# FFN down-projections as seven half-size products, one normalised and split input per FFN, two weight sums by adding transfers, the embedding in the second FFN

## The chip, the cores and the metric

The kernel runs on one core of one Trainium2 chip. The metric is the time of one execution on the device, in microseconds (us); the time of a kernel is the median of its runs. Five engines work side by side: PE (matrix products; its weight loads are listed apart as PEld), DVE and POOL (elementwise), ACT (copies, scalings and functions) and SP (issues transfers). Tiles are 128 partitions high; "128x512" is 128 partitions by 512 float32 numbers.

## The reference

One decoder layer on 512 tokens of width 1024, in float32: a first feed-forward half step, a token mixer, a second feed-forward half step, and a gated embedding. Cut to what the change touches:

```python
def rmsnorm(x, g):
    return x * lax.rsqrt(jnp.mean(x * x, axis=-1, keepdims=True) + EPS) * g

def swiglu(h, w_gu, w_down):              # w_gu 1024 x 5632, w_down 2816 x 1024
    g, u = jnp.split(h @ w_gu, 2, axis=-1)
    return (jax.nn.silu(g) * u) @ w_down

x = x + 0.5 * swiglu(rmsnorm(x, ffn1_norm[i]), ffn1_wgu[i], ffn1_wdown[i])
...
x = x + merged @ w_out[i]                 # attention, convolution and their gates
x = x + 0.5 * swiglu(rmsnorm(x, ffn2_norm[i]), ffn2_wgu[i], ffn2_wdown[i])
e = rmsnorm(p[i] @ ple_proj[i], ple_norm[i])
gate = jax.nn.sigmoid(rmsnorm(x, ple_gate_norm[i]) @ ple_gate_w[i])
x = x + gate * e
```

## The kernel before

**Layout.** x lies feature-major in eight tiles `x[o]` of 128x512: features down the partitions, the 512 tokens along the row. Every product keeps float32 accuracy by splitting both sides into a high and a low part: `split_into` (line 681) makes the high part on ACT (an ACTIVATE copy with rounding, `whi`) and the low part on DVE (a subtraction, `wlo`), and `mm3` (line 708) issues three matmuls: low weights by high data, high by high, high weights by low data. A weight piece is a tile of 128x1024, loaded by one SP transfer (`raw_...`) and split.

**Stages.** In program order: the first FFN (call on line 1104), the mixer, whose steps stand in the table ORDER (line 40; K and Q projections, a and b the convolution inputs, A E V attention, g and h gates, p its projection, L a norm, e0 e1 the embedding), two projections `cp` and `wo`, the second FFN (line 1476), and the gate `pg` with the output.

**An FFN** (`ffn`, line 920) has 22 blocks of 128 hidden features. The first four (f1) or two (f2) are plain: `products` runs `f_g` and `f_u` over eight k tiles on the normalised-later input `h` (gain applied, the token norm `rb` multiplied in afterwards by `gated`). The other blocks go two at a time through `pair` (line 966): a 2 by 2 block product (two feature blocks by two halves of the model width, and the two halves of the tokens) done as seven products of half the row length instead of eight, each on a form of the weights and a form of the input, numbered 1 to 7. Weight forms 1, 2 and 4 are loaded pieces; 3, 5, 6 and 7 are sums `f_s` of pieces, made by eight "flex" additions of 128x512 per pair that the planner puts on POOL or DVE. `sums` (line 895) makes the input sums `f_t` from x before the norm is known, so each output is multiplied by `rb` after the products. One pair is 7 forms x 2 outputs (gate and up) x 4 k tiles x 3 = 168 matmuls of 128x256.

`down` (line 1059) follows after blocks 0 to 8, 8 to 16 and 16 to 22. It takes the gated blocks, split by `act_split` (line 930) into tiles of the slot class "o", and for each of the eight outputs runs 3 x 8 (or 3 x 6) matmuls of 128x512 on one weight piece (`wd`), multiplies the result by `rb` (`f_d<-f_d,f_n_rb`) and adds half of it to `x[o]`. After the last chunk, `after(o)` splits the new x for the next norm, output by output. Two FFNs have 2 x 8 x (24 + 24 + 18) = 1056 such matmuls.

**What sets the order.** The program is recorded (`record`, line 652), and a planner (`passes`, `simulate`, lines 624 and 396) lists it out per engine with its own cost table (line 297), a due time for each instruction and a fixed number of slots per class of tile (SLOTS, line 649: 54 general "a", 4 "o", three each of raw weights, high and low parts, 8 PSUM banks, two "k"). Transfers are issued by SP when a raw slot is free. Each engine then runs its list in order, with semaphores between engines.

## Time and profile before

| | |
|---|---|
| runs | 1175.85, 1176.26, 1173.57 us; median 1175.85 |
| span of the profiled execution | 1172.4 us |
| PE, DVE, ACT, POOL busy | 1161.6, 973.4, 639.7, 456.2 us |
| matmuls of 128x512 and 128x256 in the order of PE | 3262 and 3288 |
| DMA engines, mean | 98 GB/s, 115.30 MB in all |

The profiled execution's own time isn't listed apart from its span; the median of the runs is 3.45 us above the span, and that difference stands for what lies around the span. The granted TensorE clock is at nine tenths or more in each of the 40 slices of the span. All instructions bear one line (L1522, the planner's emission loop), so groups are told apart by tile names: `f_d` is a down-projection's output, `wlo_wgu`/`whi_wgu` the parts of up-projection weights, `wlo_wd`/`whi_wd` those of down-projection weights, `f_s` weight sums, `f_t` input sums, `f_g` and `f_u` gate and up.

### The profile page before, as it was taken

How to read it: one execution, taken by the hardware profiler on the slowest of the kernel's cores; microseconds unless marked ns; L12 is line 12 of the kernel's file. 1: busy time of each engine (PE TensorE's matmuls, PEld its weight loads, DVE VectorE, ACT ScalarE, POOL GpSimd, SP SyncE). 2: the span in 40 equal slices, each digit the busy share in tenths (PEclk: the TensorE clock that was granted, in tenths of full speed). 3: DMA queues.
4: the chain of work that ended last, by engine and by line, in shares of the span. 5: the costliest groups of instructions: out<-in, count | busy, mean ns of one | idle time of the engine just before them, and what ended most of it. 6: DMA issues, size and time to landing. Idle time of an engine off the chain costs nothing.

```text
span 1172.4 us, 17962 instructions
## 1 busy us (share of the span) xinstructions
PE 1161.6 (99%) x6740; PEld 1029.6 (88%) x6740; DVE 973.4 (83%) x1481; ACT 639.7 (55%) x1139; POOL 456.2 (39%) x418
## 2 busy tenths in 40 slices
...
GB/s 226 146 85 96 126 75 106 99 136 76 82 104 100 90 91 37 108 55 72 76 89 106 88 94 93 105 96 102 107 104 132 74 86 100 121 127 41 104 108 72
DMA packets 37815, 115.30 MB, mean 98 GB/s; under 512 B 4704, under 2 KB 9440, under 8 KB 37728
## 3 DMA queue, kind: packets, MB, share of 16 engines
...
q10 hardware_dynamic: 144, 0.03, 0.0%
...
## 4 chain that ended last, share of the span: by engine, by line
PE 94%; ACT 2%; DVE 2%; POOL 1%; issue 1%; DMA 0%; SPq 0%; DVEq 0%; ACTq 0%
PE f_d L1522 20%; PE ap L1522 4%; PE ga L1522 4%; PE pg L1522 4%; PE cp L1522 4%; PE wo L1522 4%; PE ca L1522 3%; PE gb L1522 3%; PE cb L1522 3%; PE f_u L1522 2%; PE f_g L1522 2%; PE q1b L1522 2%; PE q0b L1522 2%; PE sc L1522 2%; PE f_u14b L1522 1%; PE f_u20b L1522 1%
## 5 line engine op out<-in xcount | busy, mean ns | idle before, releaser
L1522 POOL TENSOR_TENSOR f_s<-raw_wgu,raw_wgu 128x512 f32<-128x512 f32 x51 | 86.6, 1710 | 345.5 <-DMA raw_wgu<-in_wgu 115.6
L1522 POOL TENSOR_TENSOR y<-y,ct 128x507 f32<-128x507 f32 (+27 forms) x90 | 119.1, 1343 | 6.2 <-ACT ct L1522 4.6
L1522 ACT ACTIVATE whi_wgu<-raw_wgu 128x1024 fp32r<-128x1024 f32 (+1 forms) x93 | 76.2, 834 | 81.5 <-PE f_d L1522 29.5
L1522 DVE TENSOR_TENSOR wlo_wgu<-raw_wgu,whi_wgu 128x1024 fp32r<-128x1024 f32 (+1 forms) x93 | 105.1, 1140 | 7.8 <-ACT whi_wgu L1522 7.3
L1522 DVE SCALAR_TENSOR_TENSOR cz<-u,dww,cz 128x504 f32<-128x504 f32 (+25 forms) x145 | 104.7, 732 | 2.3
L1522 ACT ACTIVATE whi_wd<-raw_wd 128x1024 fp32r<-128x1024 f32 (+1 forms) x48 | 47.4, 987 | 103.9 <-PE f_d L1522 84.6
L1522 DVE TENSOR_TENSOR f_d<-f_d,f_n_rb 128x512 f32<-128x512 f32 x48 | 33.4, 697 | 75.8 <-PE f_d L1522 75.8
L1522 DVE TENSOR_TENSOR f_wl<-f_s,f_wh 128x512 fp32r<-128x512 f32 x72 | 71.4, 1012 | 1.5 <-ACT f_wh L1522 1.0
L1522 POOL TENSOR_TENSOR f_s<-raw_wgu,f_s 128x512 f32<-128x512 f32 x31 | 52.3, 1694 | 51.6 <-DVE f_us L1522 20.6
L1522 DVE TENSOR_TENSOR wlo_wgu<-f_s,whi_wgu 128x512 fp32r<-128x512 f32 x80 | 66.3, 863 | 6.0 <-ACT whi_wgu L1522 5.8
L1522 ACT ACTIVATE whi_wgu<-f_s 128x512 fp32r<-128x512 f32 x80 | 46.6, 625 | 32.4 <-PE f_d L1522 8.9
L1522 ACT ACTIVATE ct<-u,dww 128x505 f32<-128x505 f32 (+28 forms) x90 | 58.2, 701 | 2.2 <-DVE u L1522 2.1
L1522 ACT ACTIVATE f_wh<-f_s 128x512 fp32r<-128x512 f32 x72 | 43.6, 626 | 26.6 <-DVE f_s L1522 12.9
L1522 POOL TENSOR_TENSOR f_s<-f_s,raw_wgu 128x512 f32<-128x512 f32 x31 | 49.2, 1594 | 20.8 <-DVE f_s L1522 6.0
L1522 DVE TENSOR_TENSOR wlo_wd<-raw_wd,whi_wd 128x1024 fp32r<-128x1024 f32 (+1 forms) x48 | 54.1, 1128 | 3.8 <-ACT whi_wd L1522 3.6
L1522 ACT ACTIVATE f_gs<-f_gs 128x512 f32<-128x512 f32 x44 | 27.6, 629 | 34.8 <-DVE f_gs L1522 34.4
L1522 POOL TENSOR_TENSOR f_t<-x 128x256 f32<-128x256 f32 x8 | 6.5, 807 | 86.8 <-DVE x L1522 81.6
L1522 DVE SCALAR_TENSOR_TENSOR x<-f_d,x 128x512 f32<-128x512 f32 x48 | 32.9, 689 | 1.4
L1522 DVE TENSOR_TENSOR f_s<-raw_wgu,raw_wgu 128x512 f32<-128x512 f32 x25 | 32.9, 1319 | 0.0
L1522 ACT ACTIVATE s<-s,m,q_r 128x128 f32<-128x128 f32 x64 | 31.0, 491 | 0.5 <-DVE m L1522 0.4
L1522 ACT ACTIVATE whi_wzc<-raw_wzc 128x1024 fp32r<-128x1024 f32 x16 | 17.0, 1061 | 22.3 <-issue 8.4
L1522 ACT ACTIVATE whi_wzg<-raw_wzg 128x1024 fp32r<-128x1024 f32 x16 | 17.1, 1069 | 16.9 <-PE ga L1522 5.0
...
## 6 DMA issues: line engine op xcount, KB each, us to landing
raw_wgu<-in_wgu SPq DMA_DIRECT2D x80, 512.0 KB, 3.7
raw_wd<-in_wd SPq DMA_DIRECT2D x32, 512.0 KB, 3.5
raw_wzc<-in_wzc SPq DMA_DIRECT2D x16, 512.0 KB, 3.6
raw_wzg<-in_wzg SPq DMA_DIRECT2D x16, 512.0 KB, 3.6
...
raw_wq<-in_wq SPq DMA_DIRECT2D x8, 512.0 KB, 3.6
raw_wap<-in_wap SPq DMA_DIRECT2D x8, 512.0 KB, 3.6
```

The lines of the kernel that those rows point to most:

```text
L1522: getattr(engines[op.eng], op.what)(*a, **k)
```

## The change

- **Down-projections** become 2 by 2 block products as well: two halves of the outputs (`x[o]` and `x[o+4]`) by even and odd hidden blocks by the two halves of the tokens. `unit` holds the seven forms and serves both `pair` and `down`. The hidden blocks go in groups of 4, 4 and 3 pairs, each group in two units (outputs 0, 1, 4, 5 and 2, 3, 6, 7). A unit is 7 forms x 2 x np x 3 matmuls of 128x256: 168 for np = 4 pairs and 126 for np = 3. The results go straight from PSUM into x by additions of 128x256 (seven forms give 14 per unit), with no product by `rb`.
- **The gated blocks** are no longer split one by one: `act_forms` makes their four sums per pair (`ta`, `tb`, four flex additions of 128x256) and splits the seven forms.
- **The normalised input**: `sums` now multiplies x by gain and norm (`xn`, eight per FFN), splits it once (`nh`, `nl`) and makes the sums `f_t` from it. All pair products use it, so no output needs `rb` after that, and the first pair can't start before the norm. The plain blocks still use `h`.
- **Weight sums**: of four sums per unit, two (21+22, then 11+(21)) are made by transfers that POOL issues and that add the loaded piece onto the tile in place (`accum_op`); two (`s6`, `s3`) by four flex additions of 128x512.
- **The embedding** leaves the mixer's ORDER (where it stood between p1 and p6) and is recorded in the second FFN behind the pair of blocks 18 and 19.
- **Slots and planner**: a 70, raw, hi and lo 4 each, no class "o"; a cost and a duration for POOL's transfers; three mixtures for the due times are tried; weights of `wdown` laid out on the host in blocks.

Per engine, in the order of the changed kernel against that of before: PE 2206 matmuls of 128x512 (1056 fewer) and 5136 of 128x256 (1848 more); POOL issues 62 transfers (54 of 128x1024, 8 of 128x768), where it issued none of weights; SP issues as many as before.

The order of PE at the first down-projection, before (where output 0 ends and output 1 begins; `f1_a01h` holds the high parts of blocks 4 to 7 and `f1_a00h` of blocks 0 to 3, `wd10` and `wd11` are the weights of outputs 0 and 1):

```order
L1522 MATMUL f1_d0_0_1190<-f1_a01h_1027,wlo_wd10_1039 128x512
L1522 MATMUL f1_d0_0_1190<-f1_a01h_1027,whi_wd10_1003 128x512
L1522 MATMUL f1_d0_0_1190<-f1_a01l_1054,whi_wd10_1003 128x512
L1522 MATMUL f1_d0_1_1225<-f1_a00h_604,wlo_wd11_1102 128x512
L1522 MATMUL f1_d0_1_1225<-f1_a00h_604,whi_wd11_1050 128x512
L1522 MATMUL f1_d0_1_1225<-f1_a00l_685,whi_wd11_1050 128x512
```

and PE there now, the first form of the first unit (`wd10_0`: first FFN, group at pair 0, half 0; `f1_f0_1` holds high and low part of form 1 of the pair at block 0, "x2" are the two matmuls with the high weights):

```order
L1567 MATMUL wd10_0_b0_1711<-f1_f0_1_609,wlo_wd10_0_1_1689 128x256
L1567 MATMUL wd10_0_b0_1711<-f1_f0_1_609,whi_wd10_0_1_1652 128x256 x2
L1567 MATMUL wd10_0_b0_1711<-f1_f2_1_819,wlo_wd10_0_1_1689 128x256
L1567 MATMUL wd10_0_b0_1711<-f1_f2_1_819,whi_wd10_0_1_1652 128x256 x2
L1567 MATMUL wd10_0_b0_1711<-f1_f4_1_1132,wlo_wd10_0_1_1689 128x256
L1567 MATMUL wd10_0_b0_1711<-f1_f4_1_1132,whi_wd10_0_1_1652 128x256 x2
L1567 MATMUL wd10_0_b0_1711<-f1_f6_1_1262,wlo_wd10_0_1_1689 128x256
L1567 MATMUL wd10_0_b0_1711<-f1_f6_1_1262,whi_wd10_0_1_1652 128x256 x2
```

Each step is half as long, and one unit's products run over 7 forms instead of 8 blocks.

The order of POOL around the weights of blocks 8 and 9 of the first FFN, before (`f1_s0_8` to `f1_s3_8` are the four sums of this pair, cut in halves 0 and 1):

```order
L1522 TENSOR_TENSOR f1_s0_8_0_1408<-raw_wgu18_10_1380,raw_wgu18_11_1302 128x512
L1522 TENSOR_TENSOR f1_s2_8_0_1421<-raw_wgu18_00_1314,raw_wgu18_10_1380 128x512
L1522 TENSOR_TENSOR f1_s1_8_1_1442<-f1_s0_8_1_1414,raw_wgu18_00_1314 128x512
L1522 TENSOR_TENSOR f1_s2_8_1_1463<-raw_wgu18_00_1314,raw_wgu18_10_1380 128x512
L1522 TENSOR_TENSOR f1_s3_8_0_1479<-raw_wgu18_01_1347,f1_s1_8_0_1428 128x512
L1522 TENSOR_TENSOR f1_s3_8_1_1508<-raw_wgu18_01_1347,f1_s1_8_1_1442 128x512
```

and now (DMA rows are the adding transfers; `raw_wgu18_21`, `_11`, `_12` are this pair's loaded pieces, `wgu18_s6` and `wgu18_s3` its two sums; `f1_ta`, `f1_tb` the sums of gated blocks of earlier pairs):

```order
L1567 DMA raw_wgu18_21_993<-in_wgu1 128x1024
L1567 TENSOR_TENSOR f1_tb2_1064<-f1_ta2_831,f1_us3_972 128x256
L1567 TENSOR_TENSOR f1_ta4_1115<-f1_us4_729 128x256
L1567 TENSOR_TENSOR wgu18_s6_0_1180<-raw_wgu18_21_993,raw_wgu18_11_789 128x512
L1567 TENSOR_TENSOR wgu18_s3_0_1200<-raw_wgu18_12_1011,wgu18_s6_0_1180 128x512
L1567 DMA raw_wgu18_11_789<-in_wgu1 128x1024
L1567 TENSOR_TENSOR wgu18_s3_1_1227<-raw_wgu18_12_1011,wgu18_s6_1_1188 128x512
L1567 TENSOR_TENSOR f1_ta6_1268<-f1_us6_1037 128x256
L1567 TENSOR_TENSOR f1_ta4_1115<-f1_us5_821,f1_ta4_1115 128x256
L1567 DMA raw_wgu110_21_1237<-in_wgu1 128x1024
```

Three of the four weight additions stand on POOL here (the fourth is on DVE), two transfers are issued between them, and the sums of gated blocks have come in.

The order of DVE at the start of the second FFN, before (behind the last instruction of its norm, `f2_n_dgl`; `f2_gs0` and `f2_gs1` are the plain blocks):

```order
L1522 TENSOR_TENSOR f2_s1_2_0_8215<-f2_s0_2_0_8196,raw_wgu22_00_8035 128x512
L1522 TENSOR_TENSOR f2_s2_2_1_8225<-raw_wgu22_00_8035,raw_wgu22_10_8150 128x512
L1522 TENSOR_TENSOR f2_s3_2_1_8239<-raw_wgu22_01_8089,f2_s1_2_1_8220 128x512
L1522 TENSOR_TENSOR wlo_wgu22_2_8264<-raw_wgu22_01_8089,whi_wgu22_2_8232 128x1024
L1522 TENSOR_TENSOR wlo_wgu22_5_8276<-f2_s0_2_0_8196,whi_wgu22_5_8249 128x512
L1522 TENSOR_TENSOR wlo_wgu22_5_8276<-f2_s0_2_1_8202,whi_wgu22_5_8249 128x512
L1522 TENSOR_TENSOR f2_gs0_8294<-f2_g0_8053,f2_n_rb_8256 128x512
```

and now (behind the low part of the first weights, eight `f2_xn`, and the first two `f2_nl`; `nl` are low parts of the normalised input, `f2_t1` an input sum, `wlo_wgu22_2` and `_6` weights of forms 2 and 6):

```order
L1567 TENSOR_TENSOR f2_nl2_8741<-f2_xn2_8671,f2_nh2_8680 128x256
L1567 TENSOR_TENSOR f2_nl2_8741<-f2_xn3_8678,f2_nh2_8680 128x256
L1567 TENSOR_TENSOR wlo_wgu22_2_8747<-raw_wgu22_12_8522,whi_wgu22_2_8646 128x1024
L1567 TENSOR_TENSOR f2_nl4_8754<-f2_xn4_8688,f2_nh4_8698 128x512
L1567 TENSOR_TENSOR f2_nl5_8763<-f2_xn5_8695,f2_nh5_8712 128x512
L1567 TENSOR_TENSOR f2_nl6_8770<-f2_xn6_8704,f2_nh6_8718 128x512
L1567 TENSOR_TENSOR f2_nl7_8779<-f2_xn7_8714,f2_nh7_8726 128x512
L1567 SCALAR_TENSOR_TENSOR f2_t1_0_8786<-f2_t0_0_8668,f2_xn4_8688 128x256
L1567 SCALAR_TENSOR_TENSOR f2_t1_0_8786<-f2_t0_0_8668,f2_xn5_8695 128x256
L1567 SCALAR_TENSOR_TENSOR f2_t1_1_8796<-f2_t0_1_8683,f2_xn6_8704 128x256
L1567 SCALAR_TENSOR_TENSOR f2_t1_1_8796<-f2_t0_1_8683,f2_xn7_8714 128x256
L1567 TENSOR_TENSOR wlo_wgu22_6_8807<-wgu22_s6_0_8561,whi_wgu22_6_8757 128x512
```

The normalised input now stands on DVE between the norm and the weights of the first pair; before, the weights' low parts followed the norm at once.

The diff, cut to its core:

```diff
-g1 p0 p2 g7 p3 L0 p4 h3 p7 h2 p5 p1 e0 e1 p6 h5 h0 h6
+g1 p0 p2 g7 p3 L0 p4 h3 p7 h2 p5 p1 p6 h5 h0 h6
...
+PLAIN, OWN = (4, 2), (False, False)
+DOWNS = {10: [(0, 4)], 18: [(4, 8)], 20: [(8, 11)]}
...
-SLOTS = {"a": 54, "o": 4, "raw": 3, "hi": 3, "lo": 3, "ps": 8, "k": 2, "x": 8, "c": 100000}
+SLOTS = {"a": 70, "raw": 4, "hi": 4, "lo": 4, "ps": 8, "k": 2, "x": 8, "c": 100000}
...
-    def sums(tag, gain):
+    def sums(tag, gain, rb):
         t1, t2 = slice(0, HS), slice(HS, S)
+        xn, hn = [], []
+        for k in range(KD):
+            xn.append(ftile(f"{tag}_xn{k}"))
+            nc.vector.scalar_tensor_tensor(xn[k], x[k], gain[:, k : k + 1], rb, op0=ALU.mult, op1=ALU.mult)
+            n, c = (HS, HS * (k % 2)) if k < 4 else (S, 0)
+            if c == 0:
+                new = rtile(f"{tag}_nh{k}"), rtile(f"{tag}_nl{k}")
+            hn.append([t[:, c : c + n] for t in new])
+            split_into(*hn[k], xn[k][:, 0:n])
         forms = [[] for _ in range(4)]
         for q in range(KD // 4):
             vs = [ftile(f"{tag}_t{f}_{q}") for f in range(4)]
             for j in range(2):
                 k, v = 2 * q + j, [t[:, j * HS : (j + 1) * HS] for t in vs]
-                g1, g2 = gain[:, k : k + 1], gain[:, k + 4 : k + 5]
-                nc.gpsimd.tensor_tensor(v[0], x[k][:, t2], x[k][:, t1], op=ALU.subtract)
-                nc.scalar.activation(v[0], v[0], AF.Copy, scale=g1)
-                nc.scalar.activation(v[2], x[k][:, t2], AF.Copy, scale=g1)
...
+                a, b = xn[k], xn[k + 4]
+                nc.flex.tensor_tensor(v[0], a[:, t1], a[:, t2], op=ALU.subtract)
+                nc.flex.tensor_tensor(v[2], b[:, t2], a[:, t2], op=ALU.subtract)
+                for to, less, xs in ((1, 0, t2), (3, 1, t1)):
+                    nc.vector.scalar_tensor_tensor(v[to], v[less], -1.0, b[:, xs], op0=ALU.mult, op1=ALU.subtract)
-    def ffn(tag, wgu, wdown, h, gain, ss, after, cuts, wide, plain, own):
+        return forms, hn
+    lo_, hi_ = slice(0, HS), slice(HS, S)
+    def unit(name, src, n, col, forms, own=False, first=None):
+        A = {}
+        for b, cls in ((11, "raw"), (12, "raw"), (21, "raw"), (22, "k")):
+            A[b] = nc.tile(f"raw_{name}_{b}", [P, PIECE], F32, cls)[:, 0:n]
+            nc.behind = first if b == 22 else None
+            nc.sync.dma_start(A[b], src(b))
+            nc.behind = None
+        nc.gpsimd.dma_start(A[21], src(22), accum_op=ALU.add)
+        half = n // 2
+        sm = {f: [ftile(f"{name}_s{f}_{c}")[:, 0:half] for c in range(2)] for f in (6, 3)}
+        for c in range(2):
+            s = slice(c * half, (c + 1) * half)
+            nc.flex.tensor_tensor(sm[6][c], A[21][:, s], A[11][:, s], op=ALU.add)
+            nc.flex.tensor_tensor(sm[3][c], A[12][:, s], sm[6][c], op=ALU.add)
...
+        b1, b2 = ([ps_tile(f"{name}_{b}{m}")[:, lo_] for m in range(2)] for b in "ab")
+        def times(m, f, w, to, start):
+            with nc.group(f"{name}_p{f}_{m}"):
+                for k, x_ in enumerate(forms[f]):
...
+                    mm3(to[m], wk, x_, start and k == 0, k == len(forms[f]) - 1, skip=f in (3, 4, 6, 7))
+        for f1, f2 in ((1, 2), (6, 5), (7, 3)):
+            w1, w2 = form(f1), form(f2)
+            if f1 == 1:
+                nc.gpsimd.dma_start(A[11], src(21), accum_op=ALU.add)
+            for m in range(2):
+                times(m, f1, w1, b2, f1 == 1)
+                times(m, f2, w2, b1, f2 != 3)
+                yield f1, m, b1[m], b2[m]
+        w = form(4)
+        for m in range(2):
+            times(m, 4, w, b2, False)
+            yield 4, m, b1[m], b2[m]
...
+        def act_forms(i, u0, u1):
+            t1, t2 = ftile(f"{tag}_ta{i}"), ftile(f"{tag}_tb{i}")
+            nc.flex.tensor_tensor(t1[:, lo_], u0[:, lo_], u0[:, hi_], op=ALU.subtract)
+            nc.flex.tensor_tensor(t2[:, lo_], u1[:, hi_], u0[:, hi_], op=ALU.add)
+            nc.flex.tensor_tensor(t1[:, hi_], u1[:, hi_], t1[:, lo_], op=ALU.subtract)
+            nc.flex.tensor_tensor(t2[:, hi_], t1[:, hi_], u1[:, lo_], op=ALU.subtract)
+            one = rtile(f"{tag}_f{i}_1")
+            split_into(one[:, lo_], one[:, hi_], u0[:, lo_])
+            f = {1: (one[:, lo_], one[:, hi_])}
+            for n1, n2, v, sign in ((2, 3, u1, -1.0), (5, 6, t1, None), (7, 4, t2, -1.0)):
+                hi, lo = split(f"{tag}_f{i}_{n1}", v, sign)
+                f[n1], f[n2] = ((hi[:, t], lo[:, t]) for t in (lo_, hi_))
+            acts.append(f)
...
-            add(0, A[1, 0], A[1, 1], ALU.add)
-            add(1, sm[0], A[0, 0], ALU.subtract)
-            add(3, A[0, 1], sm[1], ALU.subtract)
-            add(2, A[0, 0], A[1, 0], ALU.subtract)
...
-                    nc.vector.tensor_tensor(g[0][:, hi_], b1[m], rb[:, hi_], op=ALU.mult)
-                    nc.vector.tensor_tensor(g[1][:, hi_], g[1][:, hi_], rb[:, hi_], op=ALU.mult)
...
-        def down(k0, k1):
-            for o in range(KD):
-                w = piece(wdown, o, n=(k1 - k0) * P, off=k0 * P)
-                ps = ps_tile(f"{tag}_d{k0}_{o}")
...
-                nc.vector.tensor_tensor(ps, ps, rb, op=ALU.mult)
-                nc.vector.scalar_tensor_tensor(x[o], ps, 0.5, x[o], op0=ALU.mult, op1=ALU.add)
-                if k1 == KF:
...
+            at = unit(f"{wgu}{i}", src, PIECE, lambda k, m: k * 256 + m * P, forms, own, first)
...
+        def down(p0, p1, halves=(0, 1)):
+            np = p1 - p0
+            forms = {f: [acts[p][f] for p in range(p0, p1)] for f in range(1, 8)}
+            for oo in halves:
...
+                at = unit(f"{wdown}{p0}_{oo}", src, 2 * np * P, lambda k, m: (m * np + k) * P, forms)
+                for f, m, b1, b2 in at:
+                    o = 2 * oo + m
+                    todo = {1: ((b1, 0, lo_), (b2, 0, lo_)), 6: ((b2, 0, hi_), (b1, 1, hi_)),
+                            7: ((b2, 1, hi_), (b1, 0, hi_)), 4: ((b2, 1, lo_),)}[f]
+                    for b, low, t in todo:
+                        v = x[o + 4 * low][:, t]
+                        nc.vector.scalar_tensor_tensor(v, b, -0.5 if low else 0.5, v, op0=ALU.mult, op1=ALU.add)
+                    if p1 == KF // 2 and f in (7, 4):
+                        after(o + (f == 4) * 4)
...
+            if k == (6 if cuts > 1 else 1):
+                rp = spread(f"{tag}_n", mean_rstd(f"{tag}_n", ss.accs, D), True)
+                rb = ftile(f"{tag}_n_rb")
+                nc.scalar.copy(rb, rp)
...
+                products(i, range(4))
+                products(i, range(4, KD))
+        T, hn = sums(tag, gain, rp)
+        for i in range(plain):
             for ps in gu[i]:
                 ps.vt.late = True
             gated(i)
-        T = sums(tag, gain)
         for i in range(plain, KF, 2):
-            pair(i, T, i == plain)
-            if (i + 2) % CH == 0 or i + 2 == KF:
-                down((i + 1) // CH * CH, i + 2)
+            pair(i, T, hn)
+            for d in DOWNS.get(i, ()):
+                down(*d)
+            if mid and i == 18:
+                mid()
...
-    ffn("f2", "wgu2", "wd2", h3, g_ffn2, ss3, after4, 1, False, 2, False)
+    ffn("f2", "wgu2", "wd2", h3, g_ffn2, ss3, after4, 1, False, PLAIN[1], OWN[1], lambda: [embedding(i) for i in range(2)])
...
+    nc = bacc.Bacc("TRN2", target_bir_lowering=False, num_devices=1, dynamic_dma_scratch_size=4096)
```

234 lines of the change are left out of this document (106 added, 128 removed).

## The prediction

> **What bounds the kernel now.** I read the page's busy line and its chain first, then what PE waits for, then the chain in order of time, then busy time by stretch, and last the groups of DVE and POOL.
>
> ```profile
> span 1172.4 us, 17962 instructions
> PE 1161.6 (99%) x6740; PEld 1029.6 (88%) x6740; DVE 973.4 (83%) x1481; ACT 639.7 (55%) x1139; POOL 456.2 (39%) x418
> ...
> PE 94%; ACT 2%; DVE 2%; POOL 1%; issue 1%; DMA 0%; SPq 0%; DVEq 0%; ACTq 0%
> ```
>
> PE is busy for 1161.6 of 1172.4 us and is 94% of the chain. The longest of what PE waits for (us in total, times, longest):
>
> ```profile
> PE sc L1522 <- DVE qT_l L1522: 2.0, 1, 2.0
> PE warm L1522 <- DVE ones L1522: 1.1, 1, 1.1
> PE f_u L1522 <- ACT f_n_rb L1522: 0.7, 1, 0.7
> ```
>
> No single wait is over 2 us. So time is PE's time: fewer PE microseconds shorten the span by as much, as long as nobody who feeds PE falls behind. Who is nearest to that shows by stretch (columns: PE, PEld, DVE, ACT, POOL busy, then clock, DMA share, GB/s): a stretch of pairs, and one inside a down-projection.
>
> ```profile
> 160.00:181.00 21.00, 21.00 (x177) 21.00 (x177) 19.80 (x29) 11.36 (x21) 11.39 (x7) 1.00 0.25 77
> 217.00:252.00 35.00, 35.00 (x158) 29.04 (x157) 17.17 (x23) 8.12 (x9) 0.75 (x1) 1.00 0.38 125
> ```
>
> In pairs DVE works 19.80 of 21.00 us and PE still never rests; in the down-projection DVE works 17.17 of 35.00. The down-projections are where DVE catches up. POOL is far from full in both, and the granted clock is 1.00, so a matmul's price is the same in both kinds of stretch.
>
> **The core term.** The chain in order of time (start, length, what, count) holds the six down-projections whole, and a group of a pair:
>
> ```profile
> 93.16 43.55 PE f_d L1522 x192
> 138.13 1.44 PE f_g8a L1522 x12
> 217.48 43.55 PE f_d L1522 x192
> 321.50 32.67 PE f_d L1522 x144
> 862.01 43.55 PE f_d L1522 x192
> 944.12 1.96 DVE wlo_wgu L1522
> 986.52 43.55 PE f_d L1522 x192
> 1090.54 32.67 PE f_d L1522 x144
> ```
>
> Four of 43.55 and two of 32.67 are 239.5 us for 1056 matmuls of 128x512 (0.2268 each). A matmul of 128x256 in f_g8a is 1.44/12 = 0.120 us, more than half of 0.2268, so seven eighths of the work cost more than seven eighths of the time. The change adds 1848 of these: 1848 x 0.120 = 221.8 us. A full unit is 168 x 0.120 = 20.16 us (eight of them), a unit of three pairs 126 x 0.120 = 15.12 us (four). **Core: -239.5 + 221.8 = -17.7 us.** Everything else on PE stays in number: the plain blocks, the pairs, the mixer and the moved embedding, whose matmuls cost the same in either place.
>
> **What feeds PE.** DVE's and POOL's groups (count, then total and mean ns, then idle before):
>
> ```profile
> L1522 DVE TENSOR_TENSOR wlo_wgu<-raw_wgu,whi_wgu 128x1024 fp32r<-128x1024 f32 x61 | 92.0, 1510 | 7.6 <-ACT whi_wgu L1522 7.3
> L1522 DVE TENSOR_TENSOR wlo_wgu<-f_s,whi_wgu 128x512 fp32r<-128x512 f32 x80 | 66.3, 863 | 6.0 <-ACT whi_wgu L1522 5.8
> L1522 DVE TENSOR_TENSOR wlo_wd<-raw_wd,whi_wd 128x1024 fp32r<-128x1024 f32 x32 | 38.9, 1216 | 2.9 <-ACT whi_wd L1522 2.9
> L1522 DVE TENSOR_TENSOR f_d<-f_d,f_n_rb 128x512 f32<-128x512 f32 x48 | 33.4, 697 | 75.8 <-PE f_d L1522 75.8
> L1522 DVE SCALAR_TENSOR_TENSOR x<-f_d,x 128x512 f32<-128x512 f32 x48 | 32.9, 689 | 1.4
> L1522 DVE TENSOR_TENSOR f_s<-raw_wgu,raw_wgu 128x512 f32<-128x512 f32 x25 | 32.9, 1319 | 0.0
> L1522 DVE TENSOR_TENSOR f_t_l<-f_t,f_t_h 128x512 fp32r<-128x512 f32 x16 | 10.7, 682 | 0.8 <-ACT f_t_h L1522 0.7
> L1522 DVE TENSOR_TENSOR wlo_wgu<-raw_wgu,whi_wgu 128x256 fp32r<-128x256 f32 x32 | 13.0, 434 | 0.2
> L1522 DVE SCALAR_TENSOR_TENSOR f_t<-x,g_all,f_t 128x256 f32<-128x256 f32 x24 | 11.0, 480 | 0.1
> L1522 DVE TENSOR_TENSOR wlo_wgate<-raw_wgate,whi_wgate 128x1024 fp32r<-128x1024 f32 x8 | 9.8, 1219 | 1.1 <-ACT whi_wgate L1522 1.1
> L1522 DVE TENSOR_TENSOR f_us<-f_us,f_gs 128x512 f32<-128x512 f32 x19 | 15.1, 796 | 0.3
> L1522 DVE SCALAR_TENSOR_TENSOR pg_h_l<-x,g_all,pg_h_h 128x512 fp32r<-128x512 f32 x8 | 5.9, 743 | 0.4 <-ACT pg_h_h L1522 0.4
> L1522 POOL TENSOR_TENSOR f_s<-raw_wgu,raw_wgu 128x512 f32<-128x512 f32 x51 | 86.6, 1710 | 345.5 <-DMA raw_wgu<-in_wgu 115.6
> L1522 POOL TENSOR_TENSOR f_t<-x 128x256 f32<-128x256 f32 x8 | 6.5, 807 | 86.8 <-DVE x L1522 81.6
> ```
>
> DVE now, per pair: five low parts of 128x1024 (5 x 1.51 = 7.6), four of 128x512 (4 x 0.863 = 3.5), gate and up: seven of 128x256 (7 x 0.434 = 3.0) and one of 128x512 and one of 128x256 for the products with the gate (0.80 + 0.48), splits of the gated sums (2 x 0.743 + 0.68 + 0.43 = 2.6), and about one of the eight flex operations (1.32): 19.3 us, against 20.16 of PE. So a pair of now is as full as before's stretch of 19.80 in 21.00, not fuller: the norm products and most weight additions are gone, the splits of the gated forms have come. An operation of 128x256 is 0.434 as a low part and 0.480 in an input sum; for the additions into x I take the lower, since the same addition at 128x512 is 0.689 against 0.743 of the low part of its kind. A full down unit then takes DVE 5 x 1.216 + 4 x 0.863 + 14 x 0.434 = 15.6 us of 20.16, a rest of 4.5 us (3.9 at 0.480). Six down stages gave DVE about half their time before; 12 units give it a fifth to a quarter now. In all DVE goes up by some 35 us: 168 additions of 128x256 into x (168 x 0.434 = 73) and more low parts, less 33.4 + 32.9 for `f_d` and `x` and less the norm products. It stays under PE, at some 1008 of 1160. POOL had 113 of the 152 weight additions, six a pair; it has 99 in 31 units now, three a unit, and takes the `ta`/`tb` (up to 4 x 0.807 = 3.2 us a pair) and 62 issues. ACT gains splits, and at 55% has room. The multiplication of the embedding by its norm (eight, 8 x 0.743 = 5.9 us) moves to the gate stage, behind products of `pg`, on a DVE that has no pair there.
>
> **The places where PE may newly wait.** (a) Start of the second FFN: behind the norm DVE makes eight `xn` (8 x 0.689 = 5.5), their low parts (4 x 0.434 + 4 x 0.682 = 4.5), one low part of weights (1.51), four input sums (4 x 0.480 = 1.9), and two weight halves with two splits (2 x 0.863 + 2 x 0.682 = 3.1): 16.5 us until form 6. PE has beside it 16 plain groups of three matmuls of 128x512 (16 x 0.68 = 10.9) and four groups of 1.44 (5.8), 16.7 us. Next to nothing to spare, and what ACT adds between a product and its low part isn't in it: 0 to 3 us, I take 1. (b) First FFN: the same chain, but the plain blocks 2 and 3 stand between: 0 to 2, I take 0.7. (c) Gate: x3, x6, x7 are completed in the last unit's last two forms instead of one by one; the last needs an addition (0.48), a split on ACT and a low part (0.743) after PE's last product, of which the six matmuls of the first two k tiles of `pg` (6 x 0.227 = 1.4) and those of other finished tiles cover part: 0 to 3, I take 1.3. (d) Steady units: the chain of before has one wait of 1.96 us for a low part in 19 pairs; now 31 units go through the same slots. I take one more, 2.0; bounds -2 (none at all) and +22 (below). **Added waits: 1 + 0.7 + 1.3 + 2.0 = 5.0.**
>
> **The adding transfers.** No transfer of before adds or is issued by POOL. Loads of SP:
>
> ```profile
> raw_wgu<-in_wgu SPq DMA_DIRECT2D x80, 512.0 KB, 3.7
> raw_wd<-in_wd SPq DMA_DIRECT2D x32, 512.0 KB, 3.5
> ```
>
> In the order of POOL the load 21 += 22 of `wgu18` stands a unit ahead: PE is in form 2 of the pair before and has about 15 groups of 1.44, 21.6 us, until form 6 needs the sums. From this go the load (3.7), two additions on POOL (3.4) and the split (1.06 to 2.5): some 12 us are left for the adding transfer. From 3.7 (a plain load) to 11.1 (three of them: read, read and write); I take the middle, 7.4, and so nothing on PE. Each us over 12 would fall on most of 31 units.
>
> The Trainium skill, "DMA: Bandwidth & Descriptors", section "Anatomy of one DMA — SWDGE (gpsimd) path", gives 2.0 us plus bytes over 436e3 per us for a transfer issued by POOL: 3.2 us as an estimate for 512 KB, without adding; no run here shows one yet, and by it the sum stays as it is.
>
> **Sum.** Span 1172.4 - 17.7 + 5.0 = 1159.7; the median of the runs lies 3.45 above the span, so **1163 us**, 12.8 less than 1175.85.
>
> **The rivals.**
> - *No new waits* (the 1.96 goes too): 1172.4 - 17.7 - 2 + 3.45 = 1156. For it: pairs of before run 21.00 of 21.00 on PE. Against: the start of the second FFN has no slack.
> - *DVE gives the gain back.* The price is in two low parts of 128x1024: 1219 ns beside an idle POOL (`wlo_wgate`), 1510 in pairs beside POOL's additions. If the four `ta`/`tb` of a pair each hold DVE for about 0.5 us, a pair costs 19.3 + 2.0 = 21.3 against 20.16: 1.14 x 19 = 22 us, and with (a) to (c) 1172.4 - 17.7 + 22 + 3 + 3.45 = **1183, slower**. The gain is gone from (17.7 - 3)/19 = 0.77 us a pair over 20.16; about that, with the down units' rest taking part, is *no change*, 1174 to 1178. For it: DVE's rest in down stages shrinks from half to a quarter. Against: POOL's long additions per pair halve.
> - *Transfers come late.* At 14 us each instead of 12 or less, 2 x 31 = 62 us: 1225, slower. It decides at 12 + 13/31 = 12.4 us.
> - *The change doesn't do what it says*: excluded by the order's counts (1056 fewer, 1848 more).
>
> The Trainium skill, "SBUF — State Buffer", section "Who interferes with whom", says that a DVE instruction with two SBUF inputs and a GpSimd instruction that reads SBUF exclude each other, the second waiting for the whole of the first. With the rows: 1510 against 1219 agrees in direction, but 0.29 us is far from a whole POOL addition of 1.71. By the full rule four `ta`/`tb` would hold DVE up to 3.2 us a pair (19.3 + 3.2 is 2.3 over PE, 45 us, near 1206); by the row four times 0.29 is 1.2, or 20.5 in 20.16, 6 us. I stay nearer to the row.
>
> **How the numbers follow.** About 0.3% (3.5 us) is what a measurement of this kernel can tell from no change. Forecast 1163 (1158 to 1171): 0.60; no new waits, 1156: 0.13; no change: 0.11; DVE slower, 1183: 0.08; transfers late: 0.08. Faster 0.73, same 0.11, slower 0.16. The range takes in the first three and the lower half of DVE's price: 1156 to 1180.
>
> **What would show it.** Right: PE's busy time falls by about 18 us; twelve runs of 168 or 126 matmuls of down units at 0.120; PE's wait list gains a few entries of 1 to 3 us at the norm of f2 and at `pg`; adding transfers land within 12 us. Wrong: many waits of PE for `wlo_wgu` (DVE) or for `s6` (POOL, transfer behind it); DVE at 20 of 20.16 with low parts above 1.6 us; a matmul of 128x256 in a down unit above 0.125, which alone gives back 9 us.

## The result

The changed kernel takes **1190.4 us** (1189.2 to 1191.8), the kernel before 1174.7 us: ratio 1.0137, 95% interval 1.0118 to 1.0156. It is slower, and lies above the range of the prediction (1156 to 1180). The page of the changed kernel, its span, its busy line and the kinds of transfers (packets, MB, share of 16 engines):

```profile
span 1189.0 us, 19980 instructions
PE 1157.0 (97%) x7532; PEld 1056.7 (89%) x7532; DVE 1041.3 (88%) x1582; ACT 698.0 (59%) x1248; POOL 582.4 (49%) x563
...
q1 hardware_dynamic: 37584, 114.12, 28.9%
q0 software_dynamic: 8928, 31.46, 15.9%
```

PE's busy time fell by 4.6 us only, and PE now rests for 32 us of the span where it rested for 11. What PE waits for (us in total, times, longest), the first lines:

```profile
PE sc L1567 <- DVE sga L1567: 4.9, 1, 4.9
PE wd_a L1567 <- DVE x L1567: 4.4, 3, 2.0
PE wd_b L1567 <- DVE x L1567: 2.0, 2, 1.7
PE qTp L1567 <- DVE s L1567: 2.0, 2, 1.2
PE wgu_b L1567 <- DVE f_gs L1567: 1.8, 1, 1.8
PE wgu_b L1567 <- DVE f_t_l L1567: 1.5, 2, 1.2
PE wgu_a L1567 <- DVE wlo_wgu L1567: 1.4, 3, 0.6
```

Every line shown names DVE; in the whole list no line names POOL's sums or the adding transfers. The next view is busy time by stage, before and after: first FFN, mixer, `cp` and `wo`, second FFN, gate (columns: PE, PEld, DVE, ACT, POOL, clock, DMA share, GB/s; stages cut at the start of their first matmul).

```profile
5.10:354.00 348.90, 347.93 (x2244) 318.30 (x2243) 290.49 (x425) 173.54 (x303) 115.64 (x76) 1.00 0.36 113
354.00:690.30 336.30, 333.48 (x1590) 278.96 (x1589) 297.70 (x508) 248.09 (x493) 253.44 (x280) 1.00 0.27 82
690.30:777.30 87.00, 87.00 (x385) 72.05 (x384) 64.09 (x88) 39.58 (x57) 2.96 (x4) 1.00 0.33 101
777.30:1123.00 345.70, 345.00 (x2315) 320.10 (x2314) 285.49 (x407) 161.39 (x264) 82.99 (x52) 1.00 0.31 100
```

```profile
5.10:358.10 353.00, 344.02 (x2638) 333.31 (x2639) 319.04 (x472) 199.99 (x342) 164.82 (x143) 0.99 0.59 155
358.10:691.40 333.30, 324.08 (x1532) 269.88 (x1531) 303.01 (x505) 236.54 (x494) 250.26 (x280) 0.99 0.26 84
691.40:782.00 90.60, 90.06 (x386) 71.55 (x385) 55.08 (x72) 39.34 (x53) 2.84 (x3) 1.00 0.33 100
782.00:1138.40 356.40, 350.24 (x2770) 342.57 (x2769) 320.37 (x467) 204.15 (x336) 163.96 (x134) 1.00 0.55 142
```

By stage the change is +4.1, -3.0, +3.6, +10.7 and, at the gate (49.4 to 50.6), +1.2: 16.6 us of span. Summed from start to start of PE's matmuls in the timeline: the down-projections cost 116.0 and 116.8 us instead of 119.8 each; the pairs 191.2 instead of 181.6 in the first FFN and 204.2 instead of 202.8 in the second; the embedding with its norm 12.2 in the second FFN, while the mixer, which gave up 13.05, is only 3.0 shorter. So the units gained 6.7 us of the 17.7, and four places lost more than that: the start of the pairs, the mixer, `cp`, and the ends of units.

**The start of the pairs.** DVE at the first FFN (start, length, what, count):

```profile
35.25 5.35 DVE L1567 SCALAR_TENSOR_TENSOR f_xn<-x,g_all,f_n_sp 128x512 f32<-128x512 f32 x8 [1.75 <-ACT f_n_rb L1567]
...
43.15 2.40 DVE L1567 TENSOR_TENSOR f_nl<-f_xn,f_nh 128x256 fp32r<-128x256 f32 x2
...
48.31 6.84 DVE L1567 TENSOR_TENSOR f_nl<-f_xn,f_nh 128x256 fp32r<-128x256 f32 x6
...
69.76 2.94 DVE L1567 SCALAR_TENSOR_TENSOR f_t<-f_t,f_xn 128x256 f32<-128x256 f32 x2
```

The first row of `f_nl` has two low parts (2.40 us), the second six (two of 128x256, four of 128x512), which take 6.84 us where the prediction's prices give 3.6; the two input sums take 2.94 where they give 0.96. POOL is at work in the same stretch (14.91 of the 17.00 us from 34 to 51). PE reaches the first pair at 51.0 and by 75.6 has waited six times, 5.5 us in all. The clock then drops (three stretches: PE waits, PE comes back, after that):

```profile
72.00:75.00 3.00, 1.75 (x15) 1.55 (x13) 3.00 (x5) 1.09 (x2) 0.42 (x1) 1.00 0.00 0
75.00:79.40 4.40, 3.81 (x19) 3.84 (x20) 4.40 (x9) 3.80 (x7) 0.91 (x1) 0.61 0.00 0
79.40:82.00 2.60, 2.60 (x24) 2.60 (x23) 2.60 (x4) 1.66 (x3) 2.60 (x4) 1.00 0.28 27
```

**The mixer.** DVE, then POOL, at the wait of 4.9 us at `sc`:

```profile
513.80 7.70 DVE L1567 TENSOR_TENSOR oT00l<-of,oT00h 128x128 fp32r<-128x128 f32 x1
521.42 0.18 DVE L1567 TENSOR_SCALAR q_y<-q_rs 128x32 int32<-128x32 int32 x1
521.52 0.27 DVE L1567 TENSOR_TENSOR oT00l<-of,oT00h 128x128 fp32r<-128x128 f32 x1
...
522.02 0.68 DVE L1567 TENSOR_TENSOR sga<-ga,mix_n_rb 128x512 f32<-128x512 f32 x1
```

```profile
514.57 6.78 POOL L1567 TENSOR_TENSOR y<-y,ct 128x506 f32<-128x506 f32 x6
```

One subtraction of 128x128 stands for 7.70 us on DVE; the next of its kind takes 0.27. It ends at 521.50, 0.15 us after POOL's six additions `y`, run back to back (514.57 + 6.78 = 521.35); POOL's instruction before them, a low part of 128x1024, lasted until 514.61. `sga`, behind it on DVE, is what PE waits for. Such a stand of a DVE instruction beside POOL's work is called the lockout below.

**The ends of units.** In the last group of the first FFN, DVE and then PE:

```profile
327.07 1.49 DVE L1567 TENSOR_TENSOR f_f_l<-f_ta,f_f_h 128x512 fp32r<-128x512 f32 x1
328.49 1.75 DVE L1567 TENSOR_TENSOR wlo_wd<-raw_wd,whi_wd 128x768 fp32r<-128x768 f32 x1
330.16 0.74 DVE L1567 SCALAR_TENSOR_TENSOR x<-wd_a,x 128x256 f32<-128x256 f32 x2
```

```profile
330.63 0.39 PE L1567 MATMUL wd_a<-f_f_h,wlo_wd 128*128 128x256 f32 x1 [1.97 <-DVE x L1567]
```

The seven forms go on in the same four PSUM tiles: before the next form may add to `wd_a`, DVE must have read it out into x, and this addition stands behind low parts of weights and gated sums.

### The profile page after: what moved, and what is told of

Read it like the earlier page. It is cut to its first block, busy times and chain, and to the rows that moved or that the text cites. A ratio compares the mean times of both kernels' runs of the same rounds, so it can differ in the third digit from the quotient of the medians.

```text
span 1189.0 us, 19980 instructions
## 1 busy us (share of the span) xinstructions
PE 1157.0 (97%) x7532; PEld 1056.7 (89%) x7532; DVE 1041.3 (88%) x1582; ACT 698.0 (59%) x1248; POOL 582.4 (49%) x563
## 5 line engine op out<-in xcount | busy, mean ns | idle before, releaser
L1567 PE MATMUL wgu_b<-f_t_h,wlo_wgu 128*128 128x256 f32 x456 | 130.6, 286 | 2.4 <-DVE f_gs L1567 1.8
L1567 PE MATMUL wgu_b<-f_t_l,whi_wgu 128*128 128x256 f32 x456 | 129.9, 285 | 1.5 <-DVE f_t_l L1567 1.5
L1567 PE MATMUL wgu_b<-f_t_h,whi_wgu 128*128 128x256 f32 x456 | 129.7, 284 | 0.0
L1567 POOL TENSOR_TENSOR y<-y,ct 128x509 f32<-128x509 f32 (+28 forms) x90 | 114.1, 1288 | 5.1 <-ACT ct L1567 3.8
L1567 DVE SCALAR_TENSOR_TENSOR cz<-u,dww,cz 128x486 f32<-128x486 f32 (+24 forms) x145 | 101.7, 729 | 1.1
L1567 PEld LDWEIGHTS wgu_b<-f_t_h,wlo_wgu 128*128 128x128 f32 x456 | 87.9, 193 | 3.4 <-ACT f_t_h L1567 2.0
L1567 PEld LDWEIGHTS wgu_b<-f_t_l,whi_wgu 128*128 128x128 f32 x456 | 87.9, 193 | 1.9 <-DVE f_t_l L1567 1.9
L1567 PEld LDWEIGHTS wgu_b<-f_t_h,whi_wgu 128*128 128x128 f32 x456 | 88.0, 193 | 0.0
L1567 PE MATMUL wgu_a<-f_nh,wlo_wgu 128*128 128x256 f32 x304 | 86.2, 284 | 1.1 <-DVE wlo_wgu L1567 1.1
L1567 PE MATMUL wgu_a<-f_nl,whi_wgu 128*128 128x256 f32 x304 | 86.3, 284 | 1.0 <-DVE f_nl L1567 1.0
```

Of the source, the lines that this page charges most:

```text
L1567: getattr(engines[op.eng], op.what)(*a, **k)
```

## The experiments

Every time below is a median; the kernel before ran on the same chips at 1173.3 to 1176.0 us. The stage lengths are taken from PE's timeline as above, in us, of one profile each (first FFN counted from PE's first matmul at 1.1, the gate up to the end of the span):

| kernel | time | ratio to before, 95% interval | FFN 1 | mixer | cp, wo | FFN 2 | gate |
|---|---|---|---|---|---|---|---|
| before | 1174.7 | | 352.9 | 336.3 | 87.1 | 345.7 | 49.4 |
| changed | 1190.4 | 1.0137 (1.0118 to 1.0156) | 357.0 | 333.3 | 90.5 | 356.4 | 50.6 |
| plain6 | 1182.3 | 1.0073 (1.0053 to 1.0094) | 351.0 | 333.5 | 90.5 | 356.2 | 50.9 |
| start_dve | 1193.5 | 1.0154 (1.0108 to 1.0201) | 357.4 | 333.1 | 90.5 | 361.9 | 50.6 |
| oT_pool | 1200.1 | 1.0225 (1.0204 to 1.0246) | 354.8 | 343.3 | 90.5 | 357.1 | 50.6 |
| y_dve | 1183.9 | 1.0069 (1.0046 to 1.0092) | 353.9 | 326.0 | 90.6 | 361.0 | 50.6 |
| p6_y | 1176.1 | 1.0024 (1.0007 to 1.0041) | 351.4 | 326.0 | 90.5 | 354.9 | 50.9 |
| tab_dve | 1186.7 | 1.0118 (1.0086 to 1.0150) | 352.8 | 333.4 | 90.5 | 356.0 | 50.6 |
| p6_tab | 1187.3 | 1.0103 (1.0086 to 1.0120) | 355.0 | 333.2 | 90.6 | 358.3 | 50.9 |
| flex_adds | 1268.8 | 1.0797 (1.0776 to 1.0818) | 393.1 | 337.5 | 90.8 | 390.9 | 53.8 |
| before_emb | 1191.5 | 1.0142 (1.0117 to 1.0166) | 353.3 | 332.7 | 90.7 | 364.6 | 49.4 |
| emb_back | 1210.1 | 1.0298 (1.0280 to 1.0316) | 372.7 | 343.8 | 88.0 | 349.7 | 50.7 |
| emb_back_p6 | 1202.6 | 1.0237 (1.0222 to 1.0253) | 354.3 | 352.6 | 87.1 | 354.5 | 50.2 |
| emb_spill | 1186.6 | 1.0116 (1.0071 to 1.0160) | 353.0 | 344.5 | 90.2 | 343.6 | 50.6 |
| emb_spill_p6 | 1181.4 | 1.0056 (1.0034 to 1.0078) | 349.2 | 339.2 | 90.1 | 349.6 | 50.8 |
| old_down | 1190.4 | 1.0134 (1.0112 to 1.0156) | 358.8 | 326.3 | 90.5 | 361.1 | 49.5 |
| old_down_p6 | 1185.9 | 1.0091 (1.0066 to 1.0116) | 352.9 | 329.9 | 90.5 | 361.1 | 49.7 |
| p6_y_copy | 1190.3 | 1.0131 (1.0113 to 1.0150) | 349.8 | 333.8 | 90.8 | 361.1 | 53.5 |
| spill_p6_copy | 1183.1 | 1.0072 (1.0056 to 1.0088) | 347.0 | 346.2 | 90.2 | 342.7 | 52.8 |
| p6_y_copy2 | 1181.2 | 1.0052 (1.0038 to 1.0066) | 345.5 | 333.2 | 87.0 | 358.4 | 52.2 |

A caution on the stage columns: the changed kernel and y_dve have the same order in both FFNs, and their profiles differ by 3 us in the first (two clock drops in one of them, none in the other) and 5 in the second (a wait of 2.7 us and a clock drop in the other). Stage differences below about 5 us from one profile each are no evidence.

### The start of the pairs: plain6, start_dve

```diff
-PLAIN, OWN = (4, 2), (False, False)
+PLAIN, OWN = (6, 2), (False, False)
```

> The changed kernel planned anew with six plain blocks in the first FFN instead of four (one pair fewer): 21.8 us of PE work for 20.16. Theory C (cover: the first pair waits for the norm chain on DVE): the waits of 51 to 75 us (5.9), the clock loss behind them (1.7) and about 1 of small gaps go, less 1.6: 1182 to 1185. Rival (DVE is full throughout the first FFN, so the waits move to the next units): 1189 to 1194.

Measured 1182.3, 8.1 us less. Two more plain blocks cost 22.4 us of `f_g` and `f_u`, and the pairs fell by 29.9 to 161.3 us for 1344 matmuls, which is 0.120 each: the pairs of the first FFN wait for nothing now. So it was cover, work of PE that runs beside the chain on DVE, that the start lacked.

start_dve kept the order and moved POOL's input sums and norm products to DVE, in both FFNs; POOL kept its weight sums (the edit is in the loop that emits the plan):

```diff
-            getattr(engines[op.eng], op.what)(*a, **k)
+            eng = op.eng
+            if eng == "POOL" and op.what == "tensor_tensor" and any(s in op.writes[0].vt.name for s in ("_t0_", "_t2_", "_gs")):
+                eng = "DVE"
+            getattr(engines[eng], op.what)(*a, **k)
```

> The changed kernel with its order kept, except that POOL's input sums f_t (16 of 128x256) and products f_gs by the norm (6 of 128x512) are issued by DVE. Theory L: at the first pair DVE's low parts f_nl took 1.14 us each beside them instead of 0.43 to 0.68; DVE takes 16 x 0.34 + 6 x 0.69 = 9.6 us more in both FFNs but is locked less; the waits at 51 to 75 us shrink by half or more, and with them the clock loss of 1.7: 1183 to 1188. Rival (DVE's load at the start, not the lock): the chain gets longer, 1191 to 1197.

1193.5, with single runs from 1184.6 to 1196.7: no clear difference from the changed kernel, and the first FFN is as long (357.4). The eight low parts `f_nl` did get shorter, 6.7 us added up instead of 9.7, but with the moved operations in between the input sums behind them ended at 58.2 instead of 56.5. PE's waits from 35 to 90 us are 6.2 us in all, where they were 5.5. Taking these operations off POOL doesn't mend the start; DVE has then as much more to do as it was held up.

### The lockout in the attention: oT_pool, y_dve, p6_y

oT_pool is the same kind of edit, for `eng == "DVE"` and names that start with `oT`, to POOL.

> The changed kernel (1190.4 us) with its order of instructions kept, except that the 32 low parts of the attention output (oT, 128x128) are issued by POOL where DVE issued them. Theory L (DVE is locked out while POOL runs additions back to back): oT00l took 7.70 us behind six POOL additions y, PE then waited 4.9 us at sc and ran 3.4 us at clock 0.50; on POOL this goes, and the time falls by 4.9 + 1.7 = 6.6 to about 1184 (1183 to 1186). Rival (the attention chain is late by itself, DVE would have been late with sga anyway): the wait stays under another name, 1189 to 1192.

It got slower, 1200.1, which neither forecast had. The lockout moved to the next DVE instruction with both inputs in SBUF, PE now waits 7.4 us in the attention, and a wait of 4.0 us at `ln_mb`, in the norm of the convolution, came in. DVE, then POOL, in oT_pool:

```profile
524.41 8.30 DVE L1570 TENSOR_TENSOR wlo_wzc<-raw_wzc,whi_wzc 128x1024 fp32r<-128x1024 f32 x1
```

```profile
524.04 1.28 POOL L1570 TENSOR_TENSOR y<-y,ct 128x503 f32<-128x503 f32 x1
525.26 0.47 POOL L1570 TENSOR_TENSOR oT02l<-of,oT02h 128x128 fp32r<-128x128 f32 x1
525.68 5.53 POOL L1570 TENSOR_TENSOR y<-y,ct 128x501 f32<-128x501 f32 x5
531.16 0.46 POOL L1570 TENSOR_TENSOR oT03l<-of,oT03h 128x128 fp32r<-128x128 f32 x1
```

Again DVE's instruction ends only after the run on POOL does: at 532.71, 1.1 us behind 531.62, and such a low part takes 1.2 us where nothing holds it. A longer run on POOL made it worse, so the run itself was taken apart:

```diff
...
+            if op.writes:
+                v = op.writes[0]
+                if eng == "POOL" and op.what == "tensor_tensor" and (v.vt.name, v.free()) in {("y4", 506), ("y4", 505), ("y4", 504), ("y2", 504), ("y2", 503), ("y2", 502)}:
+                    eng = "DVE"
```

> The changed kernel with its order kept, except that the six convolution additions (y, 128x502 to 128x506) that POOL ran back to back from 514.57 us, while DVE's oT00l stood for 7.70 us, are issued by DVE at their places. oT_pool only moved the lockout to wlo_wzc (8.30 us). Theory L: without the run no DVE instruction is held there; DVE takes 6 x 0.6 = 3.6 us more; the wait at sc falls from 4.9 to about 1 and the clock stays at 1.00: 1183 to 1187. Rival (DVE is simply late by its load there): the wait stays, 1189 to 1194.

1183.9, as the theory said. The first `oT00l` in y_dve:

```profile
510.78 0.97 DVE L1572 TENSOR_TENSOR oT00l<-of,oT00h 128x128 fp32r<-128x128 f32 x1
```

The wait at `sc` is gone, and the mixer is 7.3 us shorter (333.3 to 326.0) although DVE does six additions more. p6_y has both edits:

> plain6 (1182.3 us) with the same six convolution additions on DVE as in y_dve; its plan has the same lockout (oT00l 7.72 us). If the two causes are apart: 1182.3 - 6.5 = 1176 (1174 to 1178). Rival (the time saved is lost at the next lockout): 1180 to 1183.

1176.1 (ten runs): the two causes add up, 14.3 us of the 15.7 that separate the changed kernel from the one before. It is the best version found, and still 0.07% to 0.41% slower than before; that the two mends only reach the old time says that the forecast gain of 12.8 us went elsewhere.

### The sums of gated blocks: tab_dve, p6_tab

The same edit for names with `_ta` and `_tb`, from POOL to DVE.

> The changed kernel with its order kept, except that POOL's 77 sums of gated blocks (ta, tb, 128x256) are issued by DVE. Theory L: f_f_l falls from 1.09 to about 0.7 us and other low parts fall too; DVE gains about what it takes on (77 x 0.34 = 26 us): 1184 to 1190. Rival (DVE's sheer load is the bound in the first down units, 38.85 of 40 us): slower, 1194 to 1210.

> plain6 (1182.3 us) with POOL's sums of gated blocks (ta, tb) issued by DVE, order kept. tab_dve gained 4 us on the changed kernel, mostly in the first FFN. If that was the start of the pairs, which plain6 has mended already: 1181 to 1184. If it was the lock in the down units: 1177 to 1180.

tab_dve was 3.7 us faster than the changed kernel, which is not clear of the spread of its runs, and p6_tab 5.0 slower than plain6, outside both forecasts. tab_dve's time lies in its theory's range by luck: `f_f_l` from `f_ta`, which was to fall, stayed at 1.10 us. The two don't agree on a sign; whether these sums lie better on POOL or on DVE is not settled, and it isn't where the loss is.

### The adding transfers: flex_adds

```diff
-        nc.gpsimd.dma_start(A[21], src(22), accum_op=ALU.add)
...
+            nc.flex.tensor_tensor(sm[5][c], A[21][:, s], A[22][:, s], op=ALU.add)
+            nc.flex.tensor_tensor(sm[7][c], A[21][:, s], A[11][:, s], op=ALU.add)
...
-                nc.gpsimd.dma_start(A[11], src(21), accum_op=ALU.add)
```

> The changed kernel planned anew with all weight sums made by POOL and DVE (eight additions of 128x512 per unit), no adding transfers. Theory L: 124 more additions on POOL and DVE lock and load DVE further: 1200 to 1230. Rival T (the adding transfers come late; POOL waits 90 us for landings): 1180 to 1188.

1268.8, beyond what the theory gave. POOL's busy time goes from 582.4 to 749.1 us and DVE's to 1117.6. The transfers are worth 78 us in this kernel.

### The embedding: before_emb, emb_back, emb_spill

before_emb is the kernel before with only the embedding moved:

```diff
-g1 p0 p2 g7 p3 L0 p4 h3 p7 h2 p5 p1 e0 e1 p6 h5 h0 h6
+g1 p0 p2 g7 p3 L0 p4 h3 p7 h2 p5 p1 p6 h5 h0 h6
...
+            if mid and i == 18:
+                mid()
```

> The kernel before (1174.7 us) planned anew with the embedding moved into the second FFN as the change does, nothing else. Theory C (cover): its 13 us of PE work lay beside the norm chain of the convolution ahead of cp; without it cp has small waits (3.5 us in the changed kernel) and the attention is planned more tightly: 1177 to 1184. Rival (the embedding's place is free, and the mixer's 10 us and cp's 3.5 come from other parts): 1173 to 1176.

1191.5: in that kernel this move alone costs 16.8 us, more than either theory gave. The mixer loses 13 us of matmuls and becomes only 3.6 shorter. PE now waits 5.0 us there for the norm of the convolution, which the embedding had covered, and 3.3 us at `sc` (2.0 before), with a clock drop at each; PE at the first `cp` in before_emb:

```profile
687.19 0.80 PE L1524 MATMUL cp<-cv_h,wlo_wcp 128*128 128x512 f32 x1 [4.98 <-ACT cv_h L1524]
```

The second FFN grows by 18.9, 13.3 of it the embedding and 5.6 the pairs.

In the changed kernel the way back has a price in slots: eight results `es` would fill general slots through the whole second FFN. emb_back gives them slots of their own and takes them elsewhere; emb_spill stores them to HBM and loads them again at the gate.

```diff
-SLOTS = {"a": 70, "raw": 4, "hi": 4, "lo": 4, "ps": 8, "k": 2, "x": 8, "c": 100000}
+SLOTS = {"es": 8, "a": 66, "raw": 4, "hi": 3, "lo": 3, "ps": 8, "k": 2, "x": 8, "c": 100000}
```

```diff
+                nc.sync.dma_start(Dram("stash")[o], es[o])
...
+        es[o] = ftile(f"er{o}")
+        nc.sync.dma_start(es[o], Dram("stash")[o])
```

> The changed kernel planned anew with the embedding back at its place in the mixer; its eight results have slots of their own, for which the general slots go from 70 to 66 and high and low parts from 4 to 3. Theory C (cover): the second FFN loses 12.2 us of PE, cp loses its 3.4 us of small waits, the mixer grows by 6 to 10 instead of 13: 1178 to 1185. Rival (the embedding costs the same wherever it stands; the fewer slots cost something): 1190 to 1200.

> emb_back with six plain blocks in the first FFN. If the two causes (the norm chain without cover at the first pair, and the embedding's lost cover) are apart, the gain of plain6 (8 us) comes on top: emb_back less 6 to 9. Rival (one takes the other's place): within 3 us of emb_back.

> The changed kernel planned anew with the embedding at its old place in the mixer and its slots unchanged: the eight results are stored to memory on the chip's HBM by SP and loaded again at the gate, so that they hold no slots in the second FFN (emb_back had taken slots away, and its first FFN grew by 15.7 us). Theory C (cover): the second FFN is 12.2 us shorter, cp 3.4, the mixer 5 to 13 longer: 1179 to 1186. Rival (the place is free): 1188 to 1193.

> emb_spill with six plain blocks in the first FFN. If the causes are apart, 6 to 9 us under emb_spill, so 1171 to 1179, about the kernel before or under it. Rival: within 3 us of emb_spill.

emb_back took 1210.1: its first FFN, where no embedding stands, grew by 15.7 us, so it shows the price of slots, not of the embedding. emb_back_p6 took 1202.6, 7.5 less as forecast, but by luck: its first FFN is 18.4 shorter and its mixer 8.8 longer, with a wait of PE of 10.6 us for a low part of weights. emb_spill took 1186.6 (1183.4 to 1195.2), 3.8 less than the changed kernel and not clear of the spread; its second FFN is 12.8 shorter, but its mixer 11.2 longer, with a wait of 2.9 us of its own in the attention. emb_spill_p6 took 1181.4, 1.0 less than plain6.

These two comparisons flatter the way back, since the plans of emb_spill and emb_spill_p6 happen to be free of the lockout (no `oT00l` over 1.7 us), which costs the changed kernel and plain6 6.5 us. Against p6_y, which is free of it too, emb_spill_p6 is 5.3 us slower: its mixer is 13.2 longer, its second FFN only 5.3 shorter. So theory C falls for the changed kernel: with its plan of the mixer the embedding costs its full price in the old place. The small waits of `cp` stayed with the embedding back (90.2), so they aren't its lost cover alone; p6_y_copy2 has none of them (87.0) with the embedding moved. They come from the plan: in the changed kernel `cp` starts when its first input is just ready, and DVE makes one every 1.2 us, where PE takes 0.68:

```profile
691.19 0.69 DVE L1567 TENSOR_TENSOR cv_l<-y,cv_h 128x512 fp32r<-128x512 f32 x1
691.79 0.68 DVE L1567 TENSOR_TENSOR y<-y,ln_v_rb 128x512 f32<-128x512 f32 x1
692.41 0.69 DVE L1567 TENSOR_TENSOR cv_l<-y,cv_h 128x512 fp32r<-128x512 f32 x1
```

### What the units are worth: old_down, old_down_p6, p6_y_copy, spill_p6_copy, p6_y_copy2

old_down puts the down-projections of before into the changed kernel, after the blocks where they stood before (without the product by the norm, which the normalised input makes needless):

```diff
+            for o in range(KD):
+                w = piece(wdown, o, n=(k1 - k0) * P, off=k0 * P)
...
+                nc.vector.scalar_tensor_tensor(x[o], ps, 0.5, x[o], op0=ALU.mult, op1=ALU.add)
```

> The changed kernel planned anew with the down-projections as before (matmuls of 128x512, blocks split one by one; no product by the norm is needed), all else as changed. Theory N (the units pay their core term but lose two thirds of it to waits: down stages are 3.8 and 2.9 us shorter than before by the trace, where 17.7 was worked out): 1194 to 1200. Rival (the units cost more than they bring, through DVE's lost rest): 1174 to 1187.

> plain6 (1182.3 us) with the down-projections as before. Without the stall at the first pair on either side this gives the units alone: by the trace of the changed kernel they are worth 3.8 + 2.9 = 6.7 us with their waits: 1187 to 1191. Rival (with their waits gone from the start of the FFN the units are worth their 17.7): 1197 to 1201. Rival (worth nothing, as old_down against the changed kernel): 1180 to 1184.

old_down took 1190.4, no difference from the changed kernel and between its two forecasts. Its FFNs and gate are 5.4 us longer than the changed kernel's, its mixer 7.0 shorter, being planned without the lockout. old_down_p6 took 1185.9, 3.6 above plain6, which is not clear of the spread; its FFNs and gate are 5.6 us longer, its mixer 3.6 shorter. DVE is busy for 880.2 us in old_down, 161 less than with the units. So the units are worth some 4 to 7 us, by the trace of the changed kernel 6.7, and not 17.7.

Are the waits for x what is missing? ACT copies the results out of PSUM, and DVE adds them later:

```diff
-                        nc.vector.scalar_tensor_tensor(v, b, -0.5 if low else 0.5, v, op0=ALU.mult, op1=ALU.add)
+                        c = ftile(f"{tag}_xc{p0}_{f}_{o}_{low}{t.start}")[:, lo_]
+                        nc.scalar.activation(c, b, AF.Copy, scale=-0.5 if low else 0.5)
+                        nc.vector.tensor_tensor(v, c, v, op=ALU.add)
```

> p6_y (1176.1 us, 0.24% over the kernel before), planned anew with the units' results copied out of PSUM by ACT (168 copies of 128x256, with the factor of one half) and then added into x by DVE from there. Theory X (PE waits in the units because the next form goes on in the same bank and DVE's addition into x stands behind its low parts): the waits of the units for x (6.2 us in p6_y) go to ACT and mostly vanish, with a clock loss of 1.7 us or two: 1168 to 1173. Rival L (additions with both inputs outside PSUM are locked by POOL, and PE then waits for low parts instead): 1177 to 1185.

> emb_spill_p6 (1181.4 us) with the same copies by ACT. Its units waited 6.2 us for x. Theory X: 1172 to 1177. Rival L: 1181 to 1190.

In the units the theory holds. The down stages take 112.0 us in the first FFN of p6_y_copy and 111.7 in both of spill_p6_copy, where 110.9 is 924 x 0.120; without the copies they were 114.9 to 118.1. In the second FFN of p6_y_copy it is 118.2, of which 4.6 is PE's wait for `wlo_wgate` behind the last unit. In the time it fails: 1190.3 and 1183.1. Additions into x, p6_y and then p6_y_copy:

```profile
L1572 DVE SCALAR_TENSOR_TENSOR x<-wd_b,x 128x256 f32<-128x256 f32 x96 | 38.8, 416 | 7.2 <-PE wd_b L1572 6.6
```

```profile
L1574 DVE TENSOR_TENSOR x<-f_xc,x 128x256 f32<-128x256 f32 x168 | 97.5, 621 | 1.5 <-ACT f_xc L1574 1.4
```

With one input in PSUM every addition of p6_y takes 0.40 to 0.43 us. With both in SBUF the mean is 0.621, though there is no factor to apply: most take 0.41 too (the median), but single ones up to 2.62. DVE then falls behind, and the wait is at the next stage's start, as p6_y_copy's list of PE's waits shows:

```profile
PE kvb L1574 <- DVE mix_h_l L1574: 5.7, 1, 5.7
PE wgu_b L1574 <- DVE f_us L1574: 4.6, 3, 2.0
PE pg L1574 <- DVE wlo_wgate L1574: 4.6, 1, 4.6
```

p6_y_copy2 makes no copies for the last two forms of the last group (`if f in (1, 6) or p1 < KF // 2`).

> p6_y_copy with the copies left out for the last two forms (7 and 4) of each FFN's last group, whose additions the next stage waits for: in p6_y_copy the down stages fell to about 112 us, but the mixer then waited 5.7 us for mix_h_l and the gate 4.6 for wlo_wgate. Theory X (the waits at the ends come from the copied additions of the last forms): the down stages stay at 112 to 114, the ends wait 2 or less: 1170 to 1176. Rival (DVE's additions at 621 instead of 416 ns and a new plan of the attention eat it): 1177 to 1186.

1181.2: the ends wait less (3.4 and 2.4 us) and the first FFN is at its shortest, 345.5, but the pairs of the second FFN cost 4.3 more than in p6_y. The time lies in the rival's range. The gain in the units wasn't kept by these means.

## Why the prediction was wrong

**Where the time went.** The core term of -17.7 us was to be followed by 5.0 us of waits; 34.3 came, so that the span grew by 16.6. By stage, without the embedding's own matmuls: the pairs 9.6 in the first FFN and 1.4 in the second, the units 11.0 over their 221.8, the mixer 10.1, `cp` and `wo` 3.5, the gate 1.2; against these 2.5 were gained, by plain blocks (1.6) and the embedding (0.9).

**The price of a matmul was right.** In steady stretches the changed kernel's PE never rests (start and length, then PE, PEld, DVE): one with pairs, one with units.

```profile
195.00:225.00 30.00, 30.00 (x252) 30.00 (x251) 27.60 (x38) 19.14 (x33) 14.29 (x13) 1.00 0.70 169
270.00:300.00 30.00, 30.00 (x252) 30.00 (x251) 24.61 (x38) 12.54 (x16) 15.48 (x15) 1.00 0.56 132
```

252 matmuls in 30 us are 0.119 each. DVE at 27.60 of 30 is 18.5 us a pair, a little under the forecast of 19.3, and at 24.61 it is 16.5 us a unit, a little over the 15.6. The rival that a pair as such would cost more than 20.16 us on DVE did not come. PE's busy time fell by 4.6 us and not by 18 all the same: three clock drops hold 5.1, and short rests don't show in it, because a matmul of 128x256 is drawn 0.28 us long and the next can start 0.12 after it (`cp` and `wo` have 3.1 us more of busy time for the same matmuls).

**The step that failed first** is "(b) First FFN: the same chain, but the plain blocks 2 and 3 stand between: 0 to 2, I take 0.7". It was not worked out. The pairs there cost 9.6 us more, by waits and a clock drop. The eight low parts were priced at 0.434 and 0.682 each, 4.5 us, from places where POOL wasn't beside them; here they took 9.2 (2.40 + 6.84), and four products of the plain blocks, 2.6 us, stood before and between them on DVE and in no sum. plain6 shows that cover mends it. For the second FFN the same working, done step by step, gave 1 us; the waits at its start are 1.4. There POOL came to rest at 803.1 (until 809.4), and the same eight low parts took 4.8:

```profile
800.93 2.31 DVE L1567 TENSOR_TENSOR f_nl<-f_xn,f_nh 128x256 fp32r<-128x256 f32 x4
...
804.30 2.48 DVE L1567 TENSOR_TENSOR f_nl<-f_xn,f_nh 128x512 fp32r<-128x512 f32 x4
```

**A line that was misread** stands under (d), "one wait of 1.96 us for a low part in 19 pairs". The line `944.12 1.96 DVE wlo_wgu` is an instruction of DVE on the chain, not a rest of PE, which was busy for 14.92 of the 15 us from 940 to 955. So the 2.0 us for steady units and the 2 us that *no new waits* took off had no source. The 12 units, which (d) takes in, came out 11.0 us over, 9 more than it.

**A term that was missing**: the additions into x as waits of PE. They were counted as DVE's load, not as what the next form waits for. That is the larger part of what (d) lacked: of the 11.0 us by which the units exceed 221.8, the waits listed for x, `f_f_l` and `wlo_wd` hold 7.4 and a clock drop 1.7. The copies, which take the waits for x away, show it.

**The cost of DVE** was 1041 us, not 1008: the low parts of the gated sums at 0.92 to 1.10 us (0.68 to 0.74 taken) and `wlo_wd` of half a tile at 1.04 (0.863 taken). The rows of DVE's groups in the changed kernel:

```profile
L1567 DVE TENSOR_TENSOR wlo_wd<-wd_s,whi_wd 128x512 fp32r<-128x512 f32 x32 | 32.7, 1036 | 0.0
...
L1567 DVE SCALAR_TENSOR_TENSOR f_f_l<-f_us,f_f_h 128x512 fp32r<-128x512 f32 x22 | 24.0, 1102 | 0.0
L1567 DVE TENSOR_TENSOR f_f_l<-f_ta,f_f_h 128x512 fp32r<-128x512 f32 x22 | 23.4, 1088 | 0.0
```

The rival "DVE gives the gain back" had the right engine and nearly the right time (1183), but as an even excess per pair. The loss came where PE had no cover: at starts, at the ends of units, and in the attention.

**"The embedding, whose matmuls cost the same in either place"** was not weighed for what it hid. In the kernel before it did hide work: before_emb loses 16.8 us. In the changed kernel, with the lockout away on both sides, putting it back costs 5.3 us. How the 10 us that the mixer lost divide is known for 7.3 (the lockout, y_dve); the rest stays open, and so does why the planner's new order had that run of six additions: neither the move nor the finer pieces of `oT` were tried for it alone in the changed kernel. The plans of emb_spill and of old_down, made anew for other edits, don't have it.

**The mixer was taken as untouched.** The planner orders it anew with every edit, and one unlucky run cost 4.9 us and a clock drop.

The prediction priced the meeting of DVE and POOL by a mean row (1510 against 1219 ns). That mean hides two kinds of rows: the 61 low parts of 128x1024 in the kernel before run from 1.21 to 2.32 us, with a median of 1.22. And 7.70 us for an instruction of 0.27 is far outside it. The Trainium skill, "SBUF — State Buffer", section "Who interferes with whom", has a DVE instruction with two SBUF inputs and a GpSimd instruction that reads SBUF exclude each other, the second waiting for the whole of the first. The single rows bear this out, and go further: DVE stood through six instructions of POOL, not one.

**What held**: the adding transfers land in 5.6 us (7.4 taken, within 3.7 to 11.1), and no wait of PE names them; the gate's start cost 1.2 (1.3 taken); the start of the second FFN 1.4 (1 taken). The 3.45 us between span and median were in part spread: in each of the four runs of the changed kernel the time lies 1.7 us above the span.

```profile
raw_wgu<-in_wgu SPq DMA_DIRECT2D x80, 512.0 KB, 4.4
raw_wgu<-in_wgu POOLq DMA_DIRECT2D x38, 512.0 KB, 5.6
```
